# GpSimd's weight differences in pieces of 512 columns and a new order: a two-layer diffusion backbone on one core

## Chip, core and metric

The kernel runs on one core of a Trainium2 chip. The metric is the device time of one launch in microseconds; the lower the better. The kernel before was run three times for timing, and once more with a profile.

## What is computed

A backbone of two layers over 512 latent tokens and 256 context tokens, width 1024, all in 32-bit floating point. Each layer takes a shift, a scale and a gate from a conditioning vector, normalises, projects, mixes tokens by attention, gates with a SiLU path, projects out, normalises again and adds. Layer 0 uses differential attention (8 heads, two softmaxes of width 64 each), layer 1 grouped-query attention (8 query heads, 2 key heads of width 128). Cut to what matters:

```python
for i in range(DEPTH):                      # 2 layers
    shift, scale, gate = adaln(c, ada_w[i], ada_b[i])
    h = rms_norm(x, pre_g[i]) * (1.0 + scale) + shift
    hc = rms_norm(xc, pre_g[i]) * (1.0 + cscale) + cshift
    if i % N_MIXERS == 0:
        y, yc = diff_attention_mixer(h, hc, a_w_in[j], w_out[i], ...)   # q, k, v, z = h @ w_in
    else:
        y, yc = gqa_mixer(h, hc, b_w_in[j], w_out[i], ...)
    x = x + gate * rms_norm(y, post_g[i])
    if not last:
        xc = xc + cgate * rms_norm(yc, post_g[i])
```

## The kernel before

Every product of 32-bit numbers is made of three products of a shorter type: a value is written as a high part (`whi`, a cast on ACT) and a low part (`wlo`, the difference between the value and its high part), and `mm3` issues high x high, high x low and low x high into one PSUM bank. So for each weight tile of 128 x 1024, `wsplit` (line 783) loads `raw` through the SP queue, casts `whi` on ACT and makes `wlo` by a subtraction on GpSimd or on DVE. Which engine it is goes with the tile: the projections into the layers (28 tiles of layer 0 in the stream, and four half tiles and two whole ones in the first microseconds by `w_split`, line 1127, and `v_split`, line 1134; 18 tiles of layer 1) go to GpSimd, the output projections and two tiles of layer 1 to DVE. `raw` has two buffers, and the split pairs have three slots and one or two more in some stages, so the next load starts when a slot comes free.

The function `pieces` (line 777) makes the difference. On DVE it is one instruction over the whole width. On GpSimd it is cut into pieces of 256 columns:

```python
n = w // -(-w // 256) if eng is nc.gpsimd else w
for i in range(0, w, n):
    eng.tensor_tensor(dst[:, i:i + n], a[:, i:i + n], b[:, i:i + n], op)
```

A whole tile is thus four instructions and a half tile two. GpSimd makes other things as well: the scaling of the exponentials by the reciprocal sums (`pp`), rotary products (`qr`), the split of queries and keys (`qk`), SiLU and gate products (`sz`, `gT`, `g`), and small powers.

The attention runs in units of 128 queries. The scores go to PSUM (`sc`), DVE takes the maximum, ACT the exponential with its sum, DVE the reciprocal, GpSimd scales the first map, DVE combines it with the second in layer 0, DVE transposes blocks of 32, and a round trip through DRAM on the SP queue completes the transposition (`dr`, `at`). Then ACT and DVE split the result (`ah`, `al`), and TensorE multiplies it by the values. The projections of later heads are put in between as filler.

The order of all instructions on all engines is planned on the host. `Plan` records each operation with a price (`price`, line 300; a GpSimd operation with two inputs is priced at 190 + 2.155 ns a column, line 350) and its dependencies, and `schedule` (line 356) simulates the queues; it also holds back DVE or GpSimd where both have two-input work in SBUF. `plan` (line 457) makes some passes, takes the best, and then applies the seeds in `MOVES` (line 102) one after another: `shift` (line 484) turns each seed into a push on the planned start of some run of operations of one engine (TensorE by groups, or one of DVE, ACT, GpSimd and SP). A last `schedule` with those keys gives the order that the real program is chained to. All operations are issued from one helper (line 519), so that every row of the profile has that line, and tiles tell the groups apart.

Of the kernel before, what the change touches and what calls it, by code (L numbers as in the profile page):

```python
# [94 lines left out]
def f32(ap):  # L95
# [3 lines left out]


RANKP = ("PE",)
MOVES = (4178473, 802159930, 966172856, 997066606, 554255254, 439650472, 784864641, 891778355, 723048149, 698580076, 8309676,
# [30 lines left out]
SLACK = 0  # L133


# [22 lines left out]
class Plan:  # L158
# [298 lines left out]
    def plan(self):  # L457
# [21 lines left out]
        side = {e: sorted((o for o in key if o.eng == e), key=lambda o: start[o]) for e in ("DVE", "ACT", "POOL", "SP")}  # L479
        for s in MOVES:  # L480
            self.shift(random.Random(s), key, groups, side)
# [124 lines left out]
def tile_backbone(  # L606
# [22 lines left out]
    nc = pl  # L629
# [146 lines left out]

    def pieces(eng, dst, a, b, op):
        w = dst.shape[-1]
        n = w // -(-w // 256) if eng is nc.gpsimd else w
        for i in range(0, w, n):  # L780
            eng.tensor_tensor(dst[:, i:i + n], a[:, i:i + n], b[:, i:i + n], op)

    def wsplit(src, eng, pool, slot, key):
        r = wp.tile([P, 1024], F32, tag="raw", name=nm("raw"), bufs=2)
        nc.sync.dma_start(r, src)
        hi, lo = w_pair(pool, slot, key)
        nc.scalar.copy(hi, r)
        pieces(eng, lo, r, f32(hi), ALU.subtract)
        return hi, lo
# [62 lines left out]
    def get_wout(layer, c, n):  # L852
        return [ws.get(k) for k in wout_keys(layer, c, n)]
# [273 lines left out]
    def w_split(half, r):  # L1127
        sl = slice(half * 512, half * 512 + 512)
        for j, (hi, lo) in enumerate((wq, wk0)):
            rj = r[:, j * 512:j * 512 + 512]  # L1130
            nc.scalar.copy(hi[:, sl], rj)
            pieces(VP[EWL[2 * half + j]], lo[:, sl], rj, f32(hi[:, sl]), ALU.subtract)

    def v_split(half, rv):
        hi, lo = wv0[half]
        nc.scalar.copy(hi, rv)
        pieces(VP[EVL[half]], lo, rv, f32(hi), ALU.subtract)
# [684 lines left out]
    for qi, (c, n) in enumerate(OUTC[:2]):  # L1822
        w = get_wout(0, c, n) if qi else w_o
# [18 lines left out]
    c, n = OUTC[2]  # L1842
    w = get_wout(0, c, n)
# [73 lines left out]
    with pl.pool("t1", "right") as t1p:  # L1917
# [309 lines left out]
        for qi, (c, n) in enumerate(OUTC1):  # L2227
            w = get_wout(1, c, n) if qi else w_o
# [152 lines left out]
```

## Time and profile before

| what | us |
|---|---|
| three timed runs, median | 743.58 |
| lowest and highest of the three | 741.79, 743.76 |
| the profiled execution | 740.91 |
| its span, first to last instruction | 739.1 |
| TensorE busy | 726.0 |
| DVE busy | 551.7 |
| ACT busy | 478.4 |
| GpSimd busy | 461.8 |

Busy times are the union of an engine's instructions. Idle time of an engine is attributed to what released its next instruction. Matmuls are pipelined and their ends are modelled. A row of instructions gives the engine, the operation, the tile written and the tiles read, the shape, the number, then the busy time, the mean duration in ns and the idle time before them with its releasers.

### The profile page before, as it was taken

The numbers are of one execution on the slowest core, as the hardware profiler recorded it, in microseconds if no ns is written. First come the engines' busy times: TensorE is split into PE (matmuls) and PEld (weight loads), VectorE is DVE, ScalarE is ACT, GpSimd is POOL, SyncE is SP. The second block draws the span as 40 slices with busy tenths as digits, with TensorE's granted clock in tenths as the row PEclk, the third lists the DMA queues.
The fourth block names the chain that finished last, engine by engine and source line by source line (L and its number), as shares of the span: only waits on it lengthen the run. The fifth ranks groups of instructions, "written<-read, shape, count | busy, mean of one in ns | idle before, by whom it ended". The sixth has DMA issues, their size and how long they took to land. (4 is left out here: it accounts for less than half of the span.)

```text
span 739.1 us, 13953 instructions
## 1 busy us (share of the span) xinstructions
PE 726.0 (98%) x5030; PEld 651.1 (88%) x5030; DVE 551.7 (75%) x882; ACT 478.4 (65%) x1085; POOL 461.8 (62%) x506
## 2 busy tenths in 40 slices
PE   7999999999999999999999999999999999999996
PEld 6789888889888889888988998899999989898986
DVE  5454897969979796688887843689666789988834
ACT  6635557876678564676749853695366678788641
POOL 4454887788598856669753311466889969665201
PEclk9999999999999999999999999999999999999999
DMA  9932446255648387473757162453437678888503
GB/s 352 407 134 100 143 132 212 96 162 184 230 142 250 127 246 216 131 228 136 228 150 229 50 236 86 144 179 115 143 129 231 175 237 244 230 259 255 154 29 114
DMA packets 52884, 133.85 MB, mean 181 GB/s; under 512 B 6608, under 2 KB 28368, under 8 KB 51280
## 3 DMA queue, kind: packets, MB, share of 16 engines
q1 hardware_dynamic: 49248, 127.82, 54.1%
q10 hardware_dynamic: 3568, 5.16, 2.2%
q8 instruction: 39, 0.64, 0.4%
q14 instruction: 29, 0.24, 0.1%
HBM read 98.61 MB, written 30.15 MB: 174 GB/s over the span
## 5 line engine op out<-in xcount | busy, mean ns | idle before, releaser
L519 PE MATMUL bk<-whi,h 128*128 128x256 f32 (+1 forms) x1184 | 244.9, 298 | 2.6 <-ACT h L519 1.3
L519 PE MATMUL bk<-h,whi 128*128 128x512 f32 (+2 forms) x832 | 222.6, 348 | 0.0
L519 POOL TENSOR_TENSOR wlo<-raw,whi 128x256 fp32r<-128x256 f32 x200 | 169.2, 869 | 53.1 <-ACT whi L519 52.2
L519 PEld LDWEIGHTS bk<-whi,h 128*128 128x128 f32 x1184 | 191.0, 189 | 11.9 <-ACT h L519 2.1
L519 PE MATMUL bk<-wlo,h 128*128 128x256 f32 (+1 forms) x592 | 174.7, 298 | 0.0
L519 PEld LDWEIGHTS bk<-h,whi 128*128 128x128 f32 x832 | 144.7, 188 | 14.9 <-issue 1.7
L519 PE MATMUL bk<-h,wlo 128*128 128x512 f32 (+2 forms) x416 | 144.1, 348 | 0.0
L519 DVE TENSOR_REDUCE sm<-sc 128x1 f32<-128x768 f32 (+1 forms) x128 | 101.9, 813 | 21.0 <-PE sc L519 14.1
L519 PEld LDWEIGHTS bk<-wlo,h 128*128 128x128 f32 x592 | 111.1, 188 | 4.0
L519 DVE TENSOR_TENSOR al<-at,ah 128x512 fp32r<-128x512 f32 x103 | 96.2, 952 | 19.2 <-ACT ah L519 11.6
L519 POOL TENSOR_SCALAR pp<-pp,sm 128x768 f32<-128x768 f32 (+1 forms) x78 | 77.5, 996 | 52.6 <-DVE sm L519 29.7
L519 PEld LDWEIGHTS bk<-h,wlo 128*128 128x128 f32 x416 | 78.3, 188 | 7.0
L519 ACT CAST whi<-raw 128x1024 fp32r<-128x1024 f32 (+1 forms) x70 | 71.7, 1025 | 17.5 <-PE bk L519 7.8
L519 ACT CAST ah<-at 128x512 fp32r<-128x512 f32 x103 | 61.6, 621 | 9.8 <-PE bk L519 5.7
L519 DVE STREAM_TRANSPOSE pp<-pp 128x1536 f32<-128x1536 f32 (+1 forms) x39 | 61.4, 1575 | 3.8 <-POOL pp L519 3.7
L519 POOL TENSOR_TENSOR sz<-sz,za 128x384 f32<-128x384 f32 (+1 forms) x24 | 30.4, 1265 | 38.3 <-ACT za L519 31.6
L519 PEld LDWEIGHTS sc<-qk,qk 64*128 64x128 f32 x480 | 37.3, 185 | 15.8 <-ACT p L519 3.2
L519 ACT ACTIVATE jk<-bk 128x128 f32<-128x128 f32 (+4 forms) x66 | 22.7, 345 | 43.9 <-PE bk L519 25.6
L519 PE MATMUL sc<-qk,qk 64*128 64x256 f32 (+1 forms) x480 | 48.4, 338 | 1.1 <-ACT p L519 1.0
L519 ACT ACTIVATE pp<-sc,sm 128x768 f32<-128x768 f32 (+1 forms) x46 | 35.5, 772 | 20.2 <-DVE sm L519 20.1
L519 DVE SCALAR_TENSOR_TENSOR pp<-p,sm,pp 128x768 f32<-128x768 f32 x32 | 43.6, 1363 | 3.2 <-POOL pp L519 2.4
L519 ACT ACTIVATE za<-za 128x384 f32<-128x384 f32 (+1 forms) x72 | 39.8, 560 | 5.2 <-DVE za L519 4.9
(213 smaller groups left out, 1353.2 us busy)
## 6 DMA issues: line engine op xcount, KB each, us to landing
dr<-pp SPq DMA_DIRECT2D x32, 768.0 KB, 4.2
at<-dr SPq DMA_DIRECT2D x128, 192.0 KB, 4.6
raw<-in_a_w SPq DMA_DIRECT2D x30, 512.0 KB, 4.4
araw<-in_ada_g SPq DMA_DIRECT2D x12, 1024.0 KB, 6.2
raw<-in_b_w SPq DMA_DIRECT2D x20, 512.0 KB, 3.7
ag<-in_ada_s SPq DMA_DIRECT2D x16, 512.0 KB, 9.5
raw<-in_w_out SPq DMA_DIRECT2D x16, 512.0 KB, 3.8
sw<-qr ACTq DMA_DIRECT2D x32, 128.0 KB, 3.1
```

What stands on the lines that cost most here:

```text
L519: self.ops.append(getattr(eng, meth)(*args, **kw))
```

## The change

In `pieces`, the width of a piece on GpSimd becomes 512 columns, so that a whole tile is two instructions and a half tile one. The list `MOVES` is replaced by another one, of 189 numbers in place of 308, so that the order on every engine is another. Nothing else differs.

```diff
 RANKP = ("PE",)
-MOVES = (4178473, 802159930, 966172856, 997066606, 554255254, 439650472, 784864641, 891778355, 723048149, 698580076, 8309676,
...
+MOVES = (948417360, 434582794, 600921943, 1036722405, 750735440, 871531662, 923277532, 962065104, 542909481, 964814042,
...
 SLACK = 0
...
     def pieces(eng, dst, a, b, op):
         w = dst.shape[-1]
-        n = w // -(-w // 256) if eng is nc.gpsimd else w
+        n = w // -(-w // 512) if eng is nc.gpsimd else w
         for i in range(0, w, n):
             eng.tensor_tensor(dst[:, i:i + n], a[:, i:i + n], b[:, i:i + n], op)
```

## Rows read from the trace of the kernel before

**Rows 1.** Busy time by stretch: stretch, length, engines (instructions), granted clock, DMA share, GB/s.

```profile
0.00:40.00 40.00, 35.42 (x254) 27.10 (x255) 19.86 (x56) 25.79 (x46) 18.26 (x31) 1.00 0.92 359
...
80.00:420.00 340.00, 338.88 (x2400) 299.45 (x2400) 282.68 (x419) 232.63 (x501) 243.15 (x222) 1.00 0.56 176
420.00:540.00 120.00, 119.58 (x855) 112.07 (x854) 78.81 (x153) 70.01 (x204) 58.98 (x86) 1.00 0.43 142
540.00:640.00 100.00, 98.92 (x684) 94.14 (x683) 78.88 (x129) 74.52 (x185) 88.66 (x108) 1.00 0.72 212
...
733.50:739.10 5.60, 0.00 (x0) 0.00 (x0) 2.09 (x5) 0.91 (x4) 0.00 (x0) 0.79 0.54 187
sum 739.10, PE 726.04 PEld 651.11 DVE 551.73 ACT 478.38 POOL 461.76; mean PE 90.75 PEld 81.39 DVE 68.97 ACT 59.80 POOL 57.72
```

**Rows 2.** Groups of matmuls that read a low part of weights.

```profile
L519 PE MATMUL bk<-wlo,h 128*128 128x256 f32 (+1 forms) x592 | 174.7, 298 | 0.0
L519 PE MATMUL bk<-h,wlo 128*128 128x512 f32 (+2 forms) x416 | 144.1, 348 | 0.0
```

**Rows 3.** Waits of TensorE: total us, times, longest.

```profile
PE sc L519 <- POOL xt L519: 1.6, 1, 1.6
...
PE sc L519 <- ACT p L519: 1.0, 2, 0.6
```

**Rows 4.** Groups of instructions on GpSimd, shapes apart.

```profile
L519 POOL TENSOR_TENSOR wlo<-raw,whi 128x256 fp32r<-128x256 f32 x200 | 169.2, 869 | 53.1 <-ACT whi L519 52.2 <-POOL wlo L519 0.3 <-PE bk L519 0.3
...
L519 POOL TENSOR_TENSOR qr<-qr,rope 128x512 f32<-128x512 f32 x14 | 23.2, 1659 | 0.2 <-DMA sw<-qr 0.2
L519 POOL TENSOR_TENSOR qr<-qr,sw 128x512 f32<-128x512 f32 x14 | 20.4, 1458 | 1.5 <-DVE sw L519 1.4
...
L519 POOL TENSOR_TENSOR ac<-gacc,ac 128x512 fp32r<-128x512 f32 x2 | 2.6, 1292 | 0.0
```

**Rows 5.** Tile `wlo` on GpSimd: shortest, median, longest in ns.

```profile
L519 POOL TENSOR_TENSOR wlo<-raw,whi x200: 721/742/1463, 13.8 to 652.7; 128x256 fp32r<-128x256 f32 x100
```

**Rows 6.** GpSimd in order of time from 540 us: start, us, what.

```profile
541.05 2.83 POOL L519 TENSOR_TENSOR wlo<-raw,whi 128x256 fp32r<-128x256 f32 x4
```

**Rows 7.** DVE's differences of maps and its combinations, by group and by instruction.

```profile
L519 DVE TENSOR_TENSOR al<-at,ah 128x512 fp32r<-128x512 f32 x103 | 96.2, 952 | 19.2 <-ACT ah L519 11.6 <-PE bk L519 6.5 <-ACT jk L519 0.4
...
L519 DVE SCALAR_TENSOR_TENSOR pp<-p,sm,pp 128x768 f32<-128x768 f32 x32 | 43.6, 1363 | 3.2 <-POOL pp L519 2.4
...
L519 DVE TENSOR_TENSOR al<-at,ah x103: 647/749/2341, 101.7 to 701.5; 128x512 fp32r<-128x512 f32 x103
...
L519 DVE SCALAR_TENSOR_TENSOR pp<-p,sm,pp x32: 1006/1077/2682, 78.1 to 391.9; 128x768 f32<-128x768 f32 x32
```

**Rows 8.** Order of time from 373.7 us on DVE, GpSimd, ACT and TensorE.

```profile
373.72 2.68 DVE L519 SCALAR_TENSOR_TENSOR pp<-p,sm,pp 128x768 f32<-128x768 f32 x1
373.76 1.84 POOL L519 TENSOR_TENSOR gT<-gT,sz 128x768 f32<-128x768 f32 x1
...
376.33 1.81 DVE L519 TENSOR_REDUCE sm<-sc 128x1 f32<-128x768 f32 x2
...
378.20 0.89 ACT L519 ACTIVATE p<-sc,sm 128x768 f32<-128x768 f32 x1
...
379.24 0.97 PE L519 MATMUL sc<-qk,qk 64*128 64x512 f32 x6 [0.61 <-ACT p L519]
```

**Rows 9.** Instructions that write or read `wlo`, from 540 to 640 us.

```profile
540.00:640.00 100.00, 36.12 (x121) 22.43 (x121) 0.00 (x0) 31.98 (x40) 1.00 0.72 212
```

**Rows 10.** The chain that ended last: start, us, what.

```profile
733.44 0.48 ACT jk L519 x2
...
735.05 0.40 DVEq L2374
```

**Rows 11.** TensorE in the first 20 us, in order of time.

```profile
9.23 1.09 PE L519 MATMUL sc<-ident,xt 128*128 128x128 f32 x8 [1.63 <-POOL xt L519]
...
17.18 0.38 PE L519 MATMUL bk<-whi,h 128*128 128x256 f32 x1 [1.32 <-ACT h L519]
```

48 rows, old and new, of the table MOVES are left out of this document.

## The prediction

> **What bounds the kernel now.** I read the table by stretches first, then the matmul groups, then who kept TensorE waiting. In [rows 1] TensorE is busy for 726.04 of 739.10 us, so 13.06 us are idle in the whole span: 40.00 - 35.42 = 4.58 in the first 40 us, 1.12 between 80 and 420, 0.42 up to 540, 1.08 up to 640, 5.60 after the last matmul, and the remaining 0.26 in the stretches left out. GpSimd is next to nowhere a bound: 461.76 us in all; only between 540 and 640 does it come near, with 88.66 of 100 us beside DVE's 78.88. The two groups of matmuls that read a low part, `wlo`, show 0.0 us of idle time before them over 1008 matmuls [rows 2]: no profiled moment exists in which TensorE stood still for a difference made by GpSimd. The list of TensorE's waits [rows 3] names GpSimd once, for `xt` (1.6 us, an input row scaled in the first 10 us, which the change does not touch); the others are ACT and DVE. So the kernel is bound by TensorE's own stream of matmuls, with a start (4.58) and an end (5.60) outside it, and 13.06 - 4.58 - 5.60 = 2.88 us of standstill between 40 and 733.5 us. The change removes no matmul.
>
> **Where the sum starts.** The profiled execution took 740.91 us, 1.81 more than its span of 739.1. The median of the three runs is 743.58, that is 2.67 above the profiled one. I work out differences in the profiled execution and put them on the median.
>
> **The pieces themselves.** The 200 pieces are 48 whole tiles of four pieces and four half tiles of two; after the change they are 48 x 2 + 4 = 100. A piece of 256 columns takes 742 ns in the median and 869 in the mean [rows 4, 5]. A GpSimd difference of 512 columns on the same types stands in the trace twice, as `ac`, at 1292 ns; with other work beside it the sum `qr<-qr,sw` of 512 columns has a mean of 1458 [rows 4]. Undisturbed, a piece less saves 2 x 742 - 1292 = 192 ns, times 100 = 19.2 us. The means give 2 x 869 - 1458 = 280 ns, 28.0 us, if the longer piece is held up as `qr` is, and 2 x 869 - 1292 = 446 ns, 44.6 us, if it is never held up. The lower end comes from pieces in a row: four take 2.83 us [rows 6], so a pair costs 1.42 and not 1.48, and a saving of 0.13 us times 100 is 13 us. I take 28 us of GpSimd time, since the pieces will go on meeting DVE as `qr` does, and keep 13 to 44.6.
>
> The Trainium skill, "Perfetto Trace Analysis", section "GPSIMD Engine Instruction", says a GpSimd span in a profile is not to be trusted and that one should go by the spacing of consecutive starts. The rows in a row agree, by a little: 1.42 us for two where two spans add up to 1.48. By that rule the term would be the 13 us, and the time would come out the same, as the next part shows.
>
> Of this saving nothing lies on the path that sets the end: what waits for `wlo` is TensorE, at 0.0 us [rows 2], and in front of `wlo` GpSimd itself idles 53.1 us, 52.2 of it for ACT's `whi` [rows 4]. The cover is the slack between a tile's landing and its first matmul. If that cover were gone, the first matmul of a tile would see the first piece 1292 - 742 = 0.55 us later than now (a matmul needs 128 or 256 columns of the tile and today waits for one piece of 256 alone). With 52 tiles the far bound is 52 x 0.55 = 28.6 us; the rows show not one tile in that position, so I take 0, and the part of it that a bad order could bring back stays with the slower rival.
>
> **What the longer piece does to DVE.** DVE's two-input operations and GpSimd's hold each other up. The row to see is at 373.72: a DVE combination of two attention maps takes 2.68 us where the shortest takes 1.006 [rows 7], because GpSimd's product `gT` of 768 columns runs from 373.76 to 375.60; the maximum behind it starts at 376.33, the exponentials end after 379.0, and TensorE, waiting for those score banks, stands still for 0.61 us until 379.24 [rows 8]. That is the one middle stall I can follow back to GpSimd. How often would a piece do the same? The differences `al` have a mean of 952 and a minimum of 647 ns, 103 x 0.305 = 31.4 us of hold-up, and the combinations 32 x (1363 - 1006) = 11.4 us [rows 7]: 43 us, of which TensorE felt at most its 2.88, 7%. The pieces occupy 169.2 us, 23% of the span, and an operation that falls into one waits half of it on average: 135 operations x 0.23 x 0.37 = 11.5 us. After the change they occupy some 129 us, 17.5%, and the half is 0.65: 135 x 0.175 x 0.65 = 15.4 us. Plus 3.9 us for DVE, 7% of it for TensorE: +0.3 us. The bounds are 0 and, if every piece in the stretch from 540 to 640 us (40 pieces [rows 9], 20 after) delayed a chain that TensorE needs by the full 0.55, +11 us.
>
> The Trainium skill, "SBUF — State Buffer", section "Who interferes with whom", has the rule that speaks against this change: a DVE operation with two inputs in SBUF and a GpSimd operation that reads SBUF cannot run together, and issue order decides which of them blocks. The stretch at 373.72 agrees: 2.68 us is the rest of GpSimd's 1.84 plus a run of about 0.8. By that rule alone, without the cover of other matmuls, a longer piece can only hurt.
>
> **The order made anew.** The list MOVES has 189 numbers in place of 308, each a seeded push on the planner's keys, so every engine's order changes: TensorE's, and those of ACT, DVE, GpSimd and the SP queue with all its loads. It changes no duration of a matmul. What it can touch is the idle time: up to 2.88 us in the middle and some of the 4.58 at the start; the 5.60 at the end is a chain of ACT, DVE and the output DMA behind the last matmul [rows 10] with no GpSimd difference in it. At the start the DMA engines are busy for 0.92 of the time [rows 1], loading what the first modulation needs; the two large stalls there wait for GpSimd's `xt` and for ACT's `h` (1.63 and 1.32 us [rows 11]), neither of which waits for a `wlo`. I count on the new order to lose the stall at 379.24, as a GpSimd with 28 us less to do gets to `gT` earlier: -0.6. I assume that it leaves the others about as they are, since their releasers are ACT and DVE. For the range I keep -4 (all 2.88, and some 1.1 of one of the two stalls at the start) and +6 (below).
>
> **Sum.** 0 (matmuls) + 0 (`wlo` ready earlier, but nobody waits) + 0.3 (DVE) - 0.6 (order) = -0.3 us. 743.58 - 0.3 = 743.3 us. In the profiled execution that is 740.6.
>
> **The rivals.** A measurement of this kernel can tell about 0.3%, that is 2.2 us: below 741.4 counts as faster, above 745.8 as slower.
>
> Faster: the middle stalls go and the start tightens. For it: GpSimd is freed of 28 us where it is nearly full (540 to 640), and every `pp` scaled there goes on to DVE and into the matmuls. Against it: most of 2.88 us has to go, and only 0.61 traces back to GpSimd. Time: 743.58 - 2.88 - 0.7 (half of one stall at the start) = 740.0.
>
> Slower: the longer hold on DVE. Place: the attention stages, where a combination or a difference on DVE meets a piece of 1.29 us, the chain of maximum, exponential and scaling slips, and TensorE reaches the scores before their banks are free, as at 379.24. It decides once the stretch has no projection matmuls left to put in between; between 540 and 640 TensorE is at 98.92 of 100 us, so that is not now the case. Price: 0.55 us each, for 5 to 10 of the 20 pieces there, is 2.8 to 5.5 us: 746.4 to 749.1. For it: the stall at 379.24 is just this, at 1.84 us. Against it: 43 us of such hold-ups have so far cost at most 2.88.
>
> The pieces do not get cheaper: each of 512 columns takes 1.74 us, being held up by DVE, and GpSimd stays at 460 us. For it: `qr<-qr,rope` has a mean of 1659 [rows 4]. Then TensorE still sees nothing: 743.6.
>
> **How the numbers follow.** The forecast, 743.3, gets 0.36; pieces that do not get cheaper, with the same outcome, 0.05; faster 0.32; slower 0.27. So faster by over 0.3% 0.32, within 0.3% 0.41, slower 0.27. The likeliest case alone spans 741.4 to 745.8. For 8 in 10, the range goes down to 738.5 (743.58 less the 4 us above, and 1 us more for the spread of the runs, 741.79 to 743.76) and up to 749.5 (743.58 + 5.5, and 0.4 for that spread), leaving some 0.1 on either side.
>
> **What would show it.** `wlo` 100 times at 1.3 to 1.5 us and GpSimd's busy time near 434 us show the first step; idle time before the matmuls that read `wlo` still at 0.0 shows the second; the mean of `al` up by no more than 0.1 us and of the combination likewise shows the third; TensorE's busy time at 726 and idle time between 40 and 733.5 us at 2 to 3 us shows the sum. I am wrong if `wlo` shows up as a releaser of TensorE (cover gone), if the idle time between 540 and 640 grows to 4 us or more with waits for DVE or for ACT behind DVE (the hold), or if the first 40 us change by over 2 us (the order of loads, which I have counted at nothing).

## The result and the profile after

The changed kernel takes 745.97 us in the median of 8 runs (744.16 to 747.93), the kernel before 742.95 in 8 (740.78 to 746.55): a ratio of 1.0047, with an interval from 1.003 to 1.0065. It is slower by about half a per cent. The profiled execution after takes 746.31 us with a span of 744.1, against 740.91 and 739.1. The two profiled executions are thus 5.4 us apart, and the medians 3.0, so not all that the two traces differ by is the change's.

(The line number that the rows carry, 507, 519, 520 or 489, is always that of the helper that records every operation; it moves with the length of the list of seeds.) The first view is the table by stretches, as in [rows 1]: stretch, length, engines (instructions), granted clock, DMA share, GB/s.

```profile
0.00:40.00 40.00, 35.08 (x261) 28.00 (x262) 20.57 (x55) 26.51 (x47) 17.72 (x26) 1.00 0.92 359
...
80.00:420.00 340.00, 338.77 (x2394) 298.50 (x2393) 283.21 (x420) 232.74 (x497) 231.53 (x172) 1.00 0.56 175
420.00:540.00 120.00, 119.82 (x857) 112.11 (x856) 79.69 (x150) 70.69 (x207) 54.51 (x72) 1.00 0.44 143
540.00:640.00 100.00, 96.72 (x658) 92.16 (x657) 76.03 (x121) 70.28 (x175) 77.94 (x84) 0.98 0.70 202
...
738.36:744.10 5.74, 0.00 (x0) 0.00 (x0) 2.13 (x6) 0.97 (x4) 0.00 (x0) 0.94 0.52 183
sum 744.10, PE 728.73 PEld 652.95 DVE 556.14 ACT 478.88 POOL 436.12; mean PE 91.09 PEld 81.62 DVE 69.52 ACT 59.86 POOL 54.52
```

TensorE's idle time is 744.10 - 728.73 = 15.37 us, 2.31 more than the 13.06 before. Nearly all of it lies in one stretch: between 540 and 640 us it is 3.28, where [rows 1] have 1.08. The first 40 us have 4.92 in place of 4.58, and the end behind the last matmul is 5.74, against 5.73 taken the same way before (the 5.60 of [rows 1] begins at 733.50). The other part of the 5.0 us of span is busy time, 728.73 - 726.04 = 2.69; the granted clock of the stretch from 540 to 640 is 0.98, which is a part of it, as shown below. GpSimd, which the change relieves, lost 461.76 - 436.12 = 25.6 us, and none of that reached the end of the kernel.

The second view is the groups of instructions, to be held against [rows 2, 4, 7].

```profile
L507 POOL TENSOR_TENSOR wlo<-raw,whi 128x512 fp32r<-128x512 f32 x100 | 141.7, 1434 | 44.1 <-ACT whi L507 41.5 <-PE bk L507 2.4
...
L507 PE MATMUL bk<-wlo,h 128*128 128x256 f32 (+1 forms) x592 | 173.6, 297 | 0.0
L507 PE MATMUL bk<-h,wlo 128*128 128x512 f32 (+2 forms) x416 | 143.3, 348 | 0.0
...
L507 DVE SCALAR_TENSOR_TENSOR pp<-p,sm,pp 128x768 f32<-128x768 f32 x32 | 42.4, 1327 | 4.3 <-POOL pp L507 3.6
...
L507 DVE TENSOR_TENSOR al<-at,ah 128x512 fp32r<-128x512 f32 x103 | 96.2, 955 | 22.2 <-ACT ah L507 20.8 <-PE bk L507 0.5 <-ACT pp L507 0.4
```

The pieces went from 169.2 to 141.7 us, the matmuls that read them still have no idle time in front, and DVE's two kinds of operations that GpSimd can hold up have means of 955 and 1327 ns, against 952 and 1363. So the pieces did what they were to do, TensorE does not wait for them, the means of DVE's operations are not up, and the kernel is slower all the same. What TensorE did wait for is in the list of its waits (total us, times, longest), beside [rows 3]:

```profile
PE sc L507 <- ACT pp L507: 2.0, 1, 2.0
PE sc L507 <- POOL xt L507: 1.6, 1, 1.6
PE bk L507 <- ACT ah L507: 1.4, 2, 1.3
```

The first and the third are new. In order of time around the first of them (start, us, engine, what, the idle time before it):

```profile
609.18 1.77 DVE L507 STREAM_TRANSPOSE pp<-pp 128x1536 f32<-128x1536 f32 x1
610.07 1.30 POOL L507 TENSOR_TENSOR sz<-sz,za 128x512 f32<-128x512 f32 x1
610.88 0.92 DVE L507 TENSOR_REDUCE sm<-sc 128x1 f32<-128x768 f32 x1
611.40 0.62 ACT L507 CAST ac<-gacc 128x512 fp32r<-128x512 f32 x1 [0.43 <-POOL sz L507]
612.12 0.97 ACT L507 ACTIVATE pp<-sc,sm,qrs 128x768 f32<-128x768 f32 x1
613.24 0.44 PE L507 MATMUL sc<-kh,qh 128*128 128x384 f32 x1 [2.00 <-ACT pp L507]
```

The scores were complete at 608.9, but the maximum over them stands behind a transposition on DVE and starts at 610.88; the exponential then stands behind a cast on ACT, which itself waited 0.43 us for `sz` of GpSimd. TensorE stood still for 2.00 us until 613.24. The other new stall is 1.25 us at 591.51, where ACT's `ah` came late after a round trip through DRAM. Together they are 3.25 of the 3.28 us of idle time in this stretch. The stall of 0.61 us at 379.24 [rows 8] is gone. Of the two new stalls only the longer one comes again where the same order runs once more: the new order with 256 columns (below) has it, with 2.00 us. The 1.25 us are missing there, and also in the kernel mended by hand, which has the pieces and the order of the changed kernel up to 609 us; so they belong to this execution.

Behind the stall of 2.00 us the granted clock falls. The same table in steps of one microsecond:

```profile
613.00:614.00 1.00, 0.76 (x4) 0.76 (x5) 1.00 (x4) 0.84 (x4) 0.00 (x0) 0.84 1.02 209
614.00:615.00 1.00, 1.00 (x7) 1.00 (x6) 1.00 (x2) 0.95 (x2) 0.91 (x1) 0.50 0.82 237
...
616.00:617.00 1.00, 1.00 (x5) 1.00 (x5) 0.00 (x0) 0.00 (x0) 0.70 (x1) 0.50 1.09 234
617.00:618.00 1.00, 1.00 (x8) 1.00 (x7) 0.46 (x1) 0.23 (x1) 0.00 (x0) 0.96 1.11 218
```

A granted clock of 0.50 is the lower of the two levels, 1.2 GHz. It holds from 613.67 to 617.09, and a pair of matmuls of 256 columns takes 0.63 us there instead of 0.40. Half of 3.4 us is 1.7 us. Not every stall of this size has it, as the last section shows, so the 1.7 us belong to this execution and are not a term for the median. Nor do they explain the 2.69 us of added busy time: the new order with 256 columns and the kernel mended by hand have no such drop between 40 and 733 us, and TensorE is busy for 728.7 and 728.5 us there all the same. Where the added busy time comes from stays open.

### The profile page after: what moved, and what is told of

Its sections match the earlier page's. It is cut to its first block, busy times and chain, and to the rows that moved or that the text cites. A ratio compares the mean times of both kernels' runs of the same rounds, so it can differ in the third digit from the quotient of the medians.

```text
span 744.1 us, 13846 instructions
## 1 busy us (share of the span) xinstructions
PE 728.7 (98%) x5030; PEld 652.9 (88%) x5030; DVE 556.1 (75%) x882; ACT 478.9 (64%) x1085; POOL 436.1 (59%) x406
## 4 chain that ended last, share of the span: by engine, by line
PE 85%; DMA 4%; DVE 4%; ACT 4%; issue 2%; POOL 1%; SPq 0%; ACTq 0%; DVEq 0%; POOLq 0%
PE bk L507 69%; PE sc L507 15%; DMA at<-dr 3%; DMA dr<-pp 1%; DVE pp L507 1%; ACT ah L507 1%; ACT za L507 1%; ACT pp L507 1%; SPq L507 0%; DVE sm L507 0%; DVE al L507 0%; ACT whi L507 0%; DVE gate L507 0%; DVE wlo L507 0%; DVE h L507 0%
## 5 line engine op out<-in xcount | busy, mean ns | idle before, releaser
L507 PEld LDWEIGHTS bk<-whi,h 128*128 128x128 f32 x1184 | 190.0, 188 | 10.3 <-issue 1.7
L507 POOL TENSOR_TENSOR wlo<-raw,whi 128x512 fp32r<-128x512 f32 x100 | 141.7, 1434 | 44.1 <-ACT whi L507 41.5
L507 POOL TENSOR_SCALAR pp<-pp,sm 128x768 f32<-128x768 f32 (+1 forms) x78 | 79.8, 1027 | 64.3 <-DVE sm L507 50.2
L507 POOL TENSOR_TENSOR sz<-sz,za 128x384 f32<-128x384 f32 (+1 forms) x24 | 27.8, 1162 | 35.0 <-ACT za L507 35.0
L507 DVE SCALAR_TENSOR_TENSOR pp<-p,sm,pp 128x768 f32<-128x768 f32 x32 | 42.4, 1327 | 4.3 <-POOL pp L507 3.6
```

Of the source, the lines that this page charges most:

```text
L507: self.ops.append(getattr(eng, meth)(*args, **kw))
```

## The experiments

Five theories were weighed; where the expectations use letters, they are these. **A**: the new order alone costs the time, whatever the width. **B**: the longer piece itself costs it. **C**: the list of seeds costs it, being shorter, or fitted worse to its own width. **D**, a sharper B that came with the second set: a tile's pieces are places in GpSimd's queue, and between two pieces of 256 columns the old order puts operations that TensorE soon needs; one piece of 512 makes these wait. The fifth is my own rival, the hold on DVE. All experiments compute the whole result; the ratio is always to the kernel before on the same chip.

**The two halves of the change, each alone.** The first keeps the order of the kernel before on every engine, and makes each pair of pieces one instruction of 512 columns at the place of the first. The second keeps the order of the changed kernel and makes each piece two of 256, one directly behind the other.

```diff
-        n = w // -(-w // 256) if eng is nc.gpsimd else w
+        wide = 512 if isinstance(pl, Emit) else 256     # second: 256, else 512
+        n = w // -(-w // wide) if eng is nc.gpsimd else w
         for i in range(0, w, n):
             eng.tensor_tensor(dst[:, i:i + n], a[:, i:i + n], b[:, i:i + n], op)
+            if isinstance(pl, Emit) and eng is nc.gpsimd:
+                pl.ops.append(pl.ops[-1])               # first: one instruction, two places
```

> The order of the kernel before on every engine, with each pair of GpSimd pieces of 256 columns made as one instruction of 512 at the place of the first. Theory A (the new order makes the loss: TensorE runs dry twice between 590 and 613 us, 1.25 and 2.00 us, and its clock is halved for 3.4 us behind the second): no loss here, 741 to 745, within 0.3% of the kernel before, TensorE's idle time between 540 and 640 us about 1 us, GpSimd busy about 434 us. Theory B (the longer pieces hold DVE up): the loss is here, ratio 1.003 to 1.008, idle time between 540 and 640 us of 3 us or more.

> The order of the changed kernel on every engine, with each GpSimd piece of 512 columns made as two of 256 one behind the other. Theory A (the order): the loss stays, ratio 1.003 to 1.008, with standstills of TensorE again near 591 and 611 us. Theory B (the pieces): the loss goes, ratio 0.998 to 1.002. If GpSimd's time were what matters in the new order, it would be slower than the changed kernel, by up to the 13 to 28 us of GpSimd time that come back: 748 or more.

Measured: 1.0072 (1.0055 to 1.009; 747.07 against 741.03 us) for the old order with 512, and 1.0067 (1.005 to 1.0084; 746.46) for the new order with 256. In one profiled execution each, the idle time of TensorE between 40 and 733.5 us is 6.10 and 4.12 us, against 2.89 before and 4.69 after. So the old order turns slow by the width alone, and A falls as the only cause. The sign that was named for B, 3 us or more of idle time between 540 and 640 us, did not come: it is 1.92 there. The new order with short pieces is no faster either, but there the two halves stand next to each other, and GpSimd's queue has nothing between them. At 512 columns the new order is at 1.0047 and the old one at 1.0072; their intervals overlap a little, so that the new order makes good a part is likely and not shown.

**The new stall, mended by hand.** In the changed kernel, DVE's maximum and two `al` are put ahead of the transposition, and ACT's exponential ahead of two casts, near 609 us.

```diff
+        for eng, at, want in [('DVE', 738, [739, 740, 741, 738]), ('ACT', 750, [752, 753, 750, 751])]:
+            ...  # permute these places of the engine's order
```

> The changed kernel with one place of its order mended: near 609 us DVE takes the maximum of a score block and the two differences behind it before a transposition that stood ahead of them, and ACT the scaled maximum and the exponential before two casts, one of which waits for GpSimd. If the standstill of 2.00 us at 611 us and the halved clock behind it (3.4 us, some 1.7 us lost) are a cause of the loss, they go, and the time is 2 to 4 us under that of the changed kernel: 742 to 744, clock of the whole run at 0.998. If the standstill only moves on (the transposed block now comes later), the time stays at 745 to 747 and another wait of TensorE of 1 us or more stands behind 611 us.

Measured: 1.0104 (1.0086 to 1.0123), 749.43 us, slower than what it was to mend, and above both ranges that were named. The profiled execution, 746.60 us, is the fastest of the six, so its trace shows only a part of the loss. The idle time in the middle is 5.22 us. The list of TensorE's waits shows where it went:

```profile
PE bk L507 <- DVE al L507: 2.2, 2, 1.5
...
PE sc L507 <- ACT pp L507: 1.5, 2, 1.1
```

In place of the 2.00 us at 611.24 there are stalls of 1.48 us at 613.2, 1.10 at 617.4, 0.73 at 610.6 and 0.61 at 621.0. The stall is not one misplaced instruction; in that stretch DVE, ACT and GpSimd all stand in the path, and moving one puts another late.

**Dose.** The old order again, with the whole tile of 1024 columns as one instruction at the first piece's place.

```diff
-        wide = 512 if isinstance(pl, Emit) else 256
+        wide = 1024 if isinstance(pl, Emit) else 256
```

> The order of the kernel before, with the differences of a whole weight tile on GpSimd as one instruction of 1024 columns, some 2.4 us, at the place of the first piece: the suspected hold doubled again. Theory A: within 0.5% of the kernel before, since TensorE has other matmuls to do meanwhile. Theory B: slower than with 512 columns in the same order, 746 to 752, and the means of DVE's two-input operations up by 0.2 us and more.

Measured: 1.0233 (1.0211 to 1.0256), 758.65 us, above the range of 746 to 752, with 12.56 us of idle time in the middle. In the same order, then, 256, 512 and 1024 columns give 1, 1.0072 and 1.0233, while GpSimd's busy time goes the other way, 461.8, 437.4 and 421.0 us. The group of pieces and three of TensorE's waits:

```profile
L519 POOL TENSOR_TENSOR wlo<-raw,whi 128x1024 fp32r<-128x1024 f32 x48 | 120.0, 2502 | 58.7 <-ACT whi L519 58.6
```

```profile
PE bk L519 <- DVE al L519: 5.1, 7, 1.6
...
PE sc L519 <- POOL gacc L519: 1.7, 1, 1.7
PE bk L519 <- POOL wlo L519: 1.5, 2, 0.9
```

At this length TensorE does wait for `wlo` by name, and for GpSimd's `gacc`; the largest part of the new waits, 5.1 us, is for `al`. The mean of `al`, 946 ns against 952 [rows 7], does not tell why; the single instructions do. GpSimd, DVE and TensorE in order of time at one of these waits:

```profile
597.39 2.38 POOL L519 TENSOR_TENSOR wlo<-raw,whi 128x1024 fp32r<-128x1024 f32 x1
597.78 2.53 DVE L519 TENSOR_TENSOR al<-at,ah 128x512 fp32r<-128x512 f32 x1
...
600.37 0.51 PE L519 MATMUL bk<-al,vh 128*128 128x256 f32 x2 [1.16 <-DVE al L519]
```

The `al` starts beside a piece and takes 2.53 us; the same one takes 0.89 us in the kernel before, and the shortest 0.647. With 0.89 it would have been done at 598.67, before TensorE's wait begins at 599.21. At 623.34, 651.29 and 669.52 it is the same: each `al` that TensorE waits for runs beside a piece of `wlo` and takes 1.99, 2.92 and 2.37 us, against 1.02, 0.68 and 0.69 before. These four waits are 3.9 of the 5.1 us. So the longer piece does hold DVE, at places that TensorE needs, though the sum over all `al` stays as it was. With 512 columns there is one such wait of 0.59 us, at 641.39: its `al` takes 1.79 us beside a piece, against 0.68 before.

**Without seeds, and with the seeds of before cut short.** `MOVES = ()` leaves each width with the order that the planner finds by itself, without any search behind it; and the kernel before gets only the first 189 of its 308 seeds.

```diff
-MOVES = (4178473, 802159930, ...
+MOVES = ()          # with 256 columns, with 512; the third keeps 256 and MOVES[:189]
```

> The kernel before with an empty list of pushes: the planner's own order for pieces of 256 columns, which no search has touched. Theory C (each list was fitted to the durations of its own pieces, and that fit is most of what the orders are worth): slower than the kernel before by 1 to 4%, 748 to 772, with standstills of TensorE of 10 us and more between 40 and 735 us. If the list were worth little, within 0.5%.

> The changed kernel with an empty list of pushes: the planner's own order for pieces of 512 columns. Beside the run with an empty list and 256 columns it tells what the longer pieces are worth when neither order was fitted. Theory B (the longer pieces cost by themselves): slower than that one by 0.3% and more. My own forecast (they are worth nothing either way): within 0.3% of it. If the saved GpSimd time were worth something: faster by 0.3% and more.

> The kernel before, pieces of 256 columns, with the first 189 of its 308 pushes: as long a list as the changed kernel has. Theory C, with the length of the list as the reason that the new order is the poorer one: slower than the kernel before by 0.3 to 1%, 743.3 to 748.5. If the last 119 pushes are worth nothing: within 0.3%.

Measured: 1.0139 (1.0104 to 1.0174; 752.58 us) with 256, 1.0196 (1.0161 to 1.023; 756.91) with 512, and 0.9988 (0.9967 to 1.0009; 741.12) with 189 seeds. The length of the list is nothing. The seeds are worth about the same to both widths: 1.0139 to 1, and 1.0196 to 1.0047, some 1.4 to 1.5%. So C falls, as far as these runs go; the new list of seeds with 256 columns, which would price that list apart from its width, was not run. What is left is the width: 756.91 - 752.58 = 4.3 us, 0.57%, with a planner that knew the width and its price, close to the 0.47% of the change itself. One pair of orders stands behind this, and how far two such orders differ by chance is not known.

**Only pairs with nothing between, and only pairs with something between.** In the old order, of the 100 pairs of pieces 65 have nothing of GpSimd's but other pieces between them, and 35 have other work. First the 65 alone are merged, then the 35 alone.

```diff
+        em.joined = {k for k, p in enumerate(pl.pairs)
+                     if all(o.n in ours for o in line[min(at[n] for n in p):max(at[n] for n in p)])}
         # second: if not all(...)
```

> The order of the kernel before; pairs of GpSimd pieces are made as one of 512 columns only where nothing but other such pieces stood between them: 65 of the 100 pairs, the other 70 pieces stay at 256. Nothing else on GpSimd waits for a piece longer than before by more than the one merged. If the loss of the same order with all pairs merged (ratio 1.0072) comes from other GpSimd work that is queued behind a merged piece (as the rotated query at 542 us, 0.94 us lost): little of it stays, ratio 0.998 to 1.003. If it comes from DVE being held up, and from the first half of a tile being ready later (as at 264 us, 0.80 us lost): most of it stays, 1.004 to 1.007.

> The order of the kernel before; only the 35 pairs of GpSimd pieces between whose halves other GpSimd work stood are made as one of 512 columns, at the place of the first half; the other 65 pairs stay as two of 256. Theory D (the gap between two pieces is what the short piece is for: other GpSimd work that TensorE needs soon goes through it): most of the loss of the same order with all pairs merged is here, ratio 1.004 to 1.007, and the rotated query near 538 us is late again by 0.8 us and more. If the length of the hold on DVE were the cause: 35% of the loss, 1.002 to 1.003.

Measured: 1.0011 (0.999 to 1.0031; 743.17 us) for the 65, no difference that can be told, and 1.004 (1.002 to 1.0061; 744.5 against 740.9) for the 35. The idle time in the middle is 3.66 and 4.96 us. The 65 took 14 us from GpSimd's busy time (448.0) and gave nothing back. In that trace TensorE waits once, for 0.5 us, on `wlo`. The 35, a third of the pairs, carry more than half of the 0.72% of merging all. Where nothing stands between, then, a longer instruction with its hold on DVE costs 0.3% at most.

**The 35 pairs moved, without a longer instruction, and merged at the other end.** In the first all 200 pieces stay at 256, and the second piece of each of the 35 pairs goes directly behind the first. In the second the 35 are merged, at the place of the second piece.

```diff
+        line = [x for o in line if o.n not in second for x in ([o, first[o.n]] if o.n in first else [o])]
+        order = [o for o in order if o.eng != "POOL"] + line        # first; no pair is merged
+        order = [o for o in order if o.n not in first]              # second; the 35 are merged
```

> The order of the kernel before with all 200 pieces at 256 columns; of the same 35 pairs the second half is moved directly behind the first, so the work that stood between them waits for it, as it waits for the merged piece. No instruction is longer than before. Theory D: slower, 1.004 to 1.008, as with those 35 merged or a little more, since two of 256 take 1.42 us against 1.29. If the length of one instruction is the cause (DVE held up for longer, the first half ready later): no loss, 0.998 to 1.002.

> As the run with the 35 pairs merged, but at the place of the second half: the work that stood between goes first, as before, and only the first half of the weights is ready later. Theory D, in the narrow form that the work in between is what matters: little loss, 0.998 to 1.003. If the matmuls that read the first half matter as much: 1.004 and more, with TensorE waiting for GpSimd's low part by name.

Measured: 1.0068 (1.0039 to 1.0097; 747.85 us) for the pieces that were only moved, and 1.0032 (1.001 to 1.0054; 744.51) for those merged at the later place. The first is the run that parts the queue from the length: no instruction is longer, GpSimd has as much to do as before (462.7 us), and the time is up as by the width itself. The second is a little above the range named for little loss, 0.998 to 1.003. One place of the first kind, GpSimd and TensorE in order of time, in the kernel before:

```profile
535.60 0.74 POOL L519 TENSOR_TENSOR wlo<-raw,whi 128x256 fp32r<-128x256 f32 x1
536.30 0.71 POOL L519 TENSOR_TENSOR qrs<-qrs,mhalf 128x2 f32<-128x2 f32 x1
536.97 0.74 POOL L519 TENSOR_TENSOR q<-ta,tb 128x256 f32<-128x256 f32 x1
537.67 1.44 POOL L519 TENSOR_TENSOR wlo<-raw,whi 128x256 fp32r<-128x256 f32 x2
...
537.91 0.38 PE L519 MATMUL bk<-ident,q 128*128 128x128 f32 x2
```

The same operations in the old order with 512 columns:

```profile
541.05 1.29 POOL L519 TENSOR_TENSOR wlo<-raw,whi 128x512 fp32r<-128x512 f32 x1
542.30 0.70 POOL L519 TENSOR_TENSOR qrs<-qrs,mhalf 128x2 f32<-128x2 f32 x1
542.97 0.72 POOL L519 TENSOR_TENSOR q<-ta,tb 128x256 f32<-128x256 f32 x1
543.75 0.44 PE L519 MATMUL bk<-ident,q 128*128 128x128 f32 x2 [0.78 <-POOL q L519]
```

And with the pieces of 256 put together:

```profile
541.05 1.43 POOL L520 TENSOR_TENSOR wlo<-raw,whi 128x256 fp32r<-128x256 f32 x2
542.44 0.71 POOL L520 TENSOR_TENSOR qrs<-qrs,mhalf 128x2 f32<-128x2 f32 x1
543.11 0.72 POOL L520 TENSOR_TENSOR q<-ta,tb 128x256 f32<-128x256 f32 x1
543.89 0.33 PE L520 MATMUL bk<-ident,q 128*128 128x128 f32 x1 [1.06 <-POOL q L520]
```

In the kernel before, `qrs` and the rotated query `q` stand between two pieces, `q` is made before TensorE comes to it, and the row of the matmuls has no idle time. With the second half put ahead of them, whether as one instruction of 1.29 us or as two in 1.43, `q` comes that much later and TensorE stands still for 0.78 and 1.06 us, with `POOL q` as the releaser. Merged at the later place, `q` is in time again, but the first half is late, and the list of waits has it by name:

```profile
PE bk L520 <- POOL wlo L520: 1.0, 2, 0.7
```

So D holds for the old order: both ends of a merged pair cost something, by different waits. It does not carry the whole loss of the moved pieces. By name TensorE waits 1.4 us there for `q` and 0.7 for `gacc`, another operation that had stood between two pieces. Half of the 7.6 us by which the profiled execution is longer falls at another place. TensorE has the same order in both, so the same matmuls can be held against each other, first in the kernel before, then with the 35 moved:

```profile
265.54 1.31 PE L519 MATMUL sc<-qk,qk 64*128 64x512 f32 x12 [0.38 <-ACT p L519]
272.18 1.68 PE L519 MATMUL sc<-qk,qk 64*128 64x512 f32 x18
...
300.63 1.07 PE L519 MATMUL bk<-araw,s 128*32 128x512 f32 x8
```

```profile
265.49 1.32 PE L520 MATMUL sc<-qk,qk 64*128 64x512 f32 x12
274.46 2.39 PE L520 MATMUL sc<-qk,qk 64*128 64x512 f32 x18 [2.45 <-ACT p L520]
...
304.38 1.06 PE L520 MATMUL bk<-araw,s 128*32 128x512 f32 x8
```

The kernel with the moved pieces is level at 265.5 us and 3.75 us behind at 304.4. The slower clock behind the wait, described in the last section, is in these 3.8 us. The old order with 512 columns loses 3.2 of its 7.4 us there: it is 1.13 us behind at the first of the three matmuls and 4.37 at the third. Behind this wait stands a load that landed late, as told below under Open. The loss does not hang on this place alone: the fastest of the seven executions with the pieces moved, 744.08 us, is still 4.1 us above the fastest of the kernel before, 740.02.

**Shorter pieces.** If shorter pieces only gave more places between them, 128 columns should be better still. No seeds, so that it stands beside the 256 above.

```diff
-MOVES = (4178473, 802159930, ...
+MOVES = ()
-        n = w // -(-w // 256) if eng is nc.gpsimd else w
+        n = w // -(-w // 128) if eng is nc.gpsimd else w
```

> The kernel before with an empty list of pushes and pieces of 128 columns, 400 of them: beside the runs with an empty list and 256 (ratio 1.0139) and 512 columns (1.0196) the third width that the planner ordered by itself. If finer pieces go on helping because the planner finds places for other GpSimd work between them (Theory D alone): 1.008 to 1.014. If GpSimd's own time counts as well (200 more instructions at some 0.15 us each in a row, 30 us): 1.014 to 1.03, so that 256 columns lie near the best width.

Measured: 1.0148 (1.0119 to 1.0178), 752.69 us, beside 752.58 with 256. The group of pieces:

```profile
L489 POOL TENSOR_TENSOR wlo<-raw,whi 128x128 fp32r<-128x128 f32 x400 | 211.7, 561 | 47.2 <-ACT whi L489 46.7
```

GpSimd pays some 42 us more than for 256 columns (169.2 in [rows 4]), and the time is the same. Either finer places are worth nothing here, or what they gain goes into the longer work; the run does not tell which.

**Taken together.** The width costs 0.7% in an order that was not made for it, 0.6% in the planner's own order, and 0.5% after the seeds. In the old order three things are shown at single places: what stands between two pieces comes late, the first half of a pair comes late, and an `al` beside a longer piece is held. How the 0.7% divides among them and the late load is not shown. That the same things are behind the 0.6% and the 0.5% is argued, not shown: an order planned for 512 has no pairs to put together again. No version ran that beats both kernels; the 0.9988 with 189 seeds can't be told from no change. **Open** stays also the one place of the old order that costs most: near 272 us a wait of scores for ACT's `p` (1.88 us with 512 columns, 1.40 with the 35 merged, 2.45 with the 35 moved, but nothing like it with the 65 or with 1024 columns) comes with a load of weights that took 10.6, 9.4 and 10.3 us there against 8.42 before. The DMA engines are busy for 0.92 to 1.14 of the time between 262 and 270 us in the run with 512 columns. ACT's cast of the loaded tile waits for the load, and the exponentials stand behind that cast. Why the load took longer was not settled, nor whether it does so in every execution of these kernels.

## Why the prediction was right and wrong

The forecast was 743.3 us and no change that can be told. The time, 745.97, lies inside the range of 738.5 to 749.5; it is on the slower side, to which I gave 0.27.

**The pieces: right.** I had 28 us less on GpSimd, and `wlo` 100 times at 1.3 to 1.5 us; measured are 169.2 - 141.7 = 27.5 us and a mean of 1434 ns. The bound of 13 us, from pieces in a row, was too low: the pieces do go on meeting DVE, as `qr` did. GpSimd's busy time came to 436.1, against the 434 I named.

**Nothing of the saving on the path: right.** The 65 pairs show it, where 14 us less for GpSimd gave 1.0011.

**The first use at 0: right for this order, not for the width.** The matmuls that read `wlo` have 0.0 us before them after the change. In the old order with 512 columns TensorE did wait for `wlo`, 0.6 us in all, and 1.0 us with the 35 merged late. The new order avoids these waits; what it gives up for that I did not ask.

**The hold on DVE, +0.3 us: right in kind, and small at this width.** `al` went up by 3 ns in the mean, the combination down by 36. Over the width in a fixed order `al` has 952, 928 and 946 ns at 256, 512 and 1024 columns. The working took 129 us for the pieces after the change where the 28 us of the part before it give 141; with 141 the term is +0.5. The Trainium skill, "SBUF — State Buffer", section "Who interferes with whom", calls the shared port pair an exclusive lock; one place of the trace after agrees, an `al` at 611.72 that takes 1.54 us beside GpSimd's `g`, which runs from 611.45 to 612.71. But that is no piece of `wlo`, and TensorE's waits in the changed kernel do not name `al`. In the old order the hold is there by name, 0.59 us at one place with 512 columns and 3.9 us at four with 1024. The means that I had named as the sign of it hide this, since a few long holds stand against many short ones. So my rival on the slower side had a real mechanism and the right stretch, 540 to 640, but one such wait and not 5 to 10; that its lower end, 746.4, is near the time measured is luck.

**The step that failed: the price of a longer piece had two terms, and needed a third.** I asked who waits for `wlo`, and whom a piece holds up on another engine. I did not ask what is queued behind the piece on GpSimd itself: `q`, `qrs`, `pp`, `gacc`, which go to ACT, DVE and TensorE within a microsecond or two. The order of time of the kernel before, shown with the 35 pairs, has two of them between its pieces, and [rows 1] have GpSimd at 88.66 of 100 us between 540 and 640, so the question could have been put from the trace of before. The second half of a pair ahead of such an operation delays it by 0.7 us, and the runs with the 35 pairs put that at 0.4 to 0.7% of the time, with the late load near 272 us in it. In place of the +0.3 us of the sum the width alone cost 6.0 us in the old order, 747.07 against 741.03. What part of the changed kernel's own 3.0 us comes this way, and what part from its new order, stays open. The count of cover was wrong for the same reason: TensorE's 0.0 us of idle time before `wlo` says that `wlo` is early, and not what it cost others on GpSimd to make it so.

**The order made anew, -0.6 us: one stall went, and larger ones came.** The stall at 379.24 did go, as I counted on. I assumed that the other stalls would stay as they were, as their releasers are ACT and DVE. Two new ones of 1.25 and 2.00 us came, with releasers on ACT; the second comes again in the new order with 256 columns, so it does not need the longer piece. Whether the order as a whole gains or loses is not shown, since no run has the new order with its width and its places in the queue apart. A releaser named at the end of a chain does not clear the engines further up: the cast ahead of that exponential had itself waited for GpSimd. My criterion for being wrong, 4 us or more of idle time between 540 and 640, was set too high: it came to 3.28 us. The first 40 us changed by 0.34 us, within what I allowed.

## What to carry to other kernels

Where an engine's order is fixed, as here, cutting an instruction into pieces buys places in its queue. Before merging such pieces, list what stands between them and how soon it is needed, and not only who waits for the pieces; the 14 us saved on GpSimd by the 65 pairs were worth nothing by themselves. To price a change of size apart from a change of order, run each size in the other's order, and once with pieces moved together at the old size: that last run shows what the queue costs with no instruction longer. To see whether a long instruction holds another engine, read the single instructions ahead of each wait: a mean over a hundred of them hid it here.

## What the runs showed of the hardware

The clock behind a stall was not expected. In the old order with the 35 pairs moved, TensorE had stood still for 2.45 us, up to 274.46, in front of these stretches:

```profile
275.00:276.00 1.00, 1.00 (x10) 0.87 (x8) 0.76 (x3) 1.00 (x3) 0.00 (x0) 0.56 0.42 33
276.00:277.00 1.00, 1.00 (x9) 0.78 (x8) 1.00 (x4) 0.27 (x1) 0.00 (x0) 0.50 0.69 160
277.00:278.00 1.00, 1.00 (x5) 1.00 (x6) 0.92 (x2) 0.00 (x0) 0.00 (x0) 0.50 0.92 221
278.00:279.00 1.00, 1.00 (x8) 1.00 (x8) 0.00 (x0) 0.00 (x0) 0.00 (x0) 0.73 1.04 428
```

TensorE is busy through all four and runs at the lower level, 1.2 GHz, for 3.4 us. The old order with 512 columns has the same behind a stall of 1.88 us, from 275.6 to 279.0, and the changed kernel behind one of 2.00 us. The new order with 256 columns has a stall of 2.00 us at 611.89, in the same place and for the same releaser, and the clock after it stays at 1.00; behind a stall of 1.40 us, with the 35 merged, it stays there too. So a stall of about 2 us was followed in some executions by another 1.7 us of slower matmuls, and in one it was not; which of the two comes was not tested. It says little about the medians: a stretch of 3.4 us at half the clock lowers the mean of a run by 0.002 (3.4 x 0.5 / 744), and the mean clock of single executions goes from 0.993 to 1.000 in 11 executions of the kernel before and from 0.995 to 0.999 in six of the same order with 512 columns, with averages of 0.9972 and 0.9968.
